# Strassen's method for most gate and up products of two FFNs in a decoder layer, and down products in three groups

## The chip, the cores and the metric

The kernel runs on one core of one Trainium2 chip. The metric is the device time of one execution in microseconds; before the change it is 1139.57 us, the median of three runs (1139.33 to 1140.59). The engines of the core are named as in the profile: PE multiplies matrices (PEld is its loading of weights), DVE, ACT and POOL work on vectors, SP issues transfers.

## The reference

One decoder layer on 512 tokens of width 1024, in float32. Two FFNs of width 2816 stand around a mixing part (two attention branches) that the change does not touch:

```python
def swiglu_ffn(x, g, w_gate, w_up, w_down):
    h = rms_norm(x, g)
    return (jax.nn.silu(h @ w_gate) * (h @ w_up)) @ w_down

x = x + 0.5 * swiglu_ffn(x, ffn1_norm, ffn1_w_gate, ffn1_w_up, ffn1_w_down)
...
x = x + merged @ w_out
x = x + 0.5 * swiglu_ffn(x, ffn2_norm, ffn2_w_gate, ffn2_w_up, ffn2_w_down)
```

## The kernel before

Everything lies transposed: a tile holds 128 features by 512 tokens. x has 8 such tiles (KD), the FFN's inner width 22 (KF). Every float32 matrix is split into a high part in PE's reduced format and the low rest, and a product of two is three matmuls (`mm3`, L110): high by high, high by low, low by high, all into one PSUM bank.

`load_w` (L97) brings a tile of weights: a transfer on SP's queue into one of three raw tiles (L104), a cast to the high part by ACT (L105), and the difference by DVE (L106; in the mixing part partly by POOL). Three buffers of high and low parts exist, so a tile can be split while two others wait or are used. PE's order is the order of the program; the other engines' instructions are put in order by the scheduler when the kernel is built.

`ffn` (L159) goes through the 22 feature tiles. For each it forms the gate product and the up product (`fm_product`, L151: 8 tiles of contraction, three matmuls of 512 columns each) against the split input `xh`, `xl`, which holds x times the gain without the norm's factor. `activate` (L165) then multiplies both by the norm's factor `rb` (L167, L170), takes the silu (L168), multiplies (L171) and splits the result into `ah` and `al` (L172, L173). PSUM has three banks for these products (`acc_tile`). The norm's statistics are computed by a few PE instructions in the second feature tile (`norm_stats`).

After all 22, the down products follow: for each of the 8 output tiles 22 x 3 matmuls, whose weights come in cuts of 8, 8 and 6 tiles (DOWN_CUTS), then half the sum is added to x (L216). In the second FFN the last output tile is done in two halves of 256 tokens, so that the first can leave while the second is computed; each finished tile is sent out at once (L770). After the first FFN each finished tile of x goes through `prep` (L115) for the mixing part.

A gate or up product and a down cut of 8 are each 24 matmuls.

Of the kernel before, what the change touches and what calls it, by code (L numbers as in the profile page):

```python
# [2 lines left out]

# [1 line left out]

# [6 lines left out]
F32 = mybir.dt.float32  # L12
F32R = mybir.dt.float32r
# [5 lines left out]
P = 128  # L19
T = 512  # L20
# [18 lines left out]
BIG = 1e30  # L39
S_W = 208  # L40
GA = ("g_ffn1", "g_mix", "g_ffn2")
DOWN_CUTS = ((0, 8), (8, 16), (16, 22))


@with_exitstack
def tile_hybrid_layer(ctx: ExitStack, tc: tile.TileContext, a: dict):
# [2 lines left out]

    ctx.enter_context(tc.manual_schedule(engines={mybir.EngineType.PE}))  # L50
    const = ctx.enter_context(tc.tile_pool(name="const", bufs=1))
    wpool = ctx.enter_context(tc.tile_pool(name="wpool", bufs=3))
    tmp = ctx.enter_context(tc.tile_pool(name="tmp", bufs=6))
    small = ctx.enter_context(tc.tile_pool(name="small", bufs=4))
# [2 lines left out]
    def acc_tile(name):  # L57
        return psum.tile([P, T], F32, tag="acc", bufs=3, name=name)
# [26 lines left out]
    hg = const.tile([P, 4], F32, name="hg")  # L85
    bf = const.tile([P, H], F32, name="bf")

    const.tile([P, 8], F32, name="before_x")
    xh = [const.tile([P, T], F32R, name=f"xh{d}") for d in range(KD)]
    xl = [const.tile([P, T], F32R, name=f"xl{d}") for d in range(KD)]  # L90
    const.tile([P, 56], F32, name="behind_x")
    ssq = [None]
    lo_eng = [V]
    first = None


    def load_w(src, n, m, raw=None):  # L97
        f = n * m
        if raw is None:
            raw = wpool.tile([P, 1024], F32, tag="raw", bufs=3, name="raw")  # L100
        wh = wpool.tile([P, 1024], F32R, tag="wh", name="wh")
        wl = wpool.tile([P, 1024], F32R, tag="wl", name="wl")
        with tc.high_priority(offset=1 if first else 30):
            nc.sync.dma_start(raw[:, :f].rearrange("p (n m) -> p n m", n=n), src)  # L104
            S.copy(wh[:, :f], raw[:, :f])  # L105
            lo_eng[0].tensor_sub(wl[:, :f], raw[:, :f], wh[:, :f].bitcast(F32))  # L106
        return (wh[:, :f].rearrange("p (n m) -> p n m", n=n),
                wl[:, :f].rearrange("p (n m) -> p n m", n=n))

    def mm3(out, lh, ll, rh, rl, start, stop):  # L110
        PE.matmul(out, lh, rh, start=start, stop=False)  # L111
        PE.matmul(out, lh, rl, start=False, stop=False)  # L112
        PE.matmul(out, ll, rh, start=False, stop=stop)  # L113

    def prep(d, gi):  # L115

        g = gains[:, gi, d:d + 1]
        S.mul(xh[d], x[d], g)
        V.scalar_tensor_tensor(xl[d], x[d], g, xh[d].bitcast(F32), op0=OP.mult, op1=OP.subtract)

# [13 lines left out]
    def norm_stats():  # L134

        ps = psum.tile([P, T], F32, tag="pt", bufs=2, name="ps_ssq")
        for t in range(NT):
            PE.matmul(ps[:, t:t + 1], ssq[0][:, t * P:(t + 1) * P], ones[:, 0:1], start=True, stop=True)
        v = small.tile([P, NT], F32, tag="v", name="v")
        V.tensor_scalar(v, ps[:, 0:NT], 1.0 / D, EPS, op0=OP.mult, op1=OP.add)  # L140
        r = small.tile([P, NT], F32, tag="rstd", bufs=2, name="rstd")
        G.tensor_tensor(r, v, nhalf[:, 0:NT], op=OP.pow)
        yield r
        pb = psum.tile([P, T], F32, tag="pt", bufs=2, name="ps_rb")
        for t in range(NT):
# [11 lines left out]
        return ps  # L157

    def ffn(n, nxt, parts=lambda d: [slice(0, T)]):  # L159
        wg, wu, wd = a[f"w_gate{n}"], a[f"w_up{n}"], a[f"w_down{n}"]  # L160
        with tc.tile_pool(name=f"ffn{n}", bufs=1) as ap:
            ah = [ap.tile([P, T], F32R, name=f"ah{n}_{f}") for f in range(KF)]
            al = [ap.tile([P, T], F32R, name=f"al{n}_{f}") for f in range(KF)]

            def activate(f, pg, pu, rb):  # L165
                g = tmp_tile("g")
                V.tensor_mul(g, pg, rb)  # L167
                S.activation(g, g, AF.Silu)  # L168
                u = tmp_tile("u")
                V.tensor_mul(u, pu, rb)  # L170
                V.tensor_mul(u, u, g)  # L171
                S.copy(ah[f], u)  # L172
                V.tensor_sub(al[f], u, ah[f].bitcast(F32))  # L173

            stats = norm_stats()
            rb = None
            held = []
            mid = {1: lambda: next(stats), 4: lambda: held.append(next(stats))}
            for f in range(KF):
                if f == 0 and first:  # L180
                    pg, pu = acc_tile("pg"), acc_tile("pu")
                    for k in range(KD):
                        for ps, w in zip((pg, pu), first):
                            PE.matmul(ps, w[k][0], xh[k], start=k == 0, stop=False)
                            PE.matmul(ps, w[k][1], xh[k], start=False, stop=False)
                            PE.matmul(ps, w[k][0], xl[k], start=False, stop=k == KD - 1)
                else:
                    pg = fm_product(load_w(wg[f], KD, P), "pg", mid if f == 1 and n == 2 else {})
                if f == 1 and n == 2:
                    activate(0, *pair0, held[0])  # L190
                    rb = held[0]
                if f == 0 and first:
                    first.clear()
                elif f == 1 and n == 1:

                    pu = fm_product(load_w(wu[f], KD, P), "pu", mid, psum.tile([P, T], F32, tag="s", bufs=2, name="pu1"))
                    activate(0, *pair0, held[0])
                    rb = held[0]
                else:
                    pu = fm_product(load_w(wu[f], KD, P), "pu")  # L200
                if f == 0:
                    pair0 = (pg, pu)
                else:
                    activate(f, pg, pu, rb)
            for d in range(KD):
                ws = []

                for cols in parts(d):
                    ps = acc_tile("pd")[:, cols]
                    for c, (lo, hi) in enumerate(DOWN_CUTS):  # L210
                        if c == len(ws):
                            ws.append(load_w(wd[d][:, lo:hi], hi - lo, P))
                        for k in range(lo, hi):
                            mm3(ps, ws[c][0][:, k - lo], ws[c][1][:, k - lo], ah[k][:, cols], al[k][:, cols],
                                k == 0, k == KF - 1)
                    V.scalar_tensor_tensor(x[d][:, cols], ps, 0.5, x[d][:, cols], op0=OP.mult, op1=OP.add)  # L216
                    nxt(d, cols)


    first = [[], []]  # L220
# [553 lines left out]
def _fm(w):  # L774

    k, n = w.shape
    return w.reshape(k // P, P, n // P, P).transpose(2, 1, 0, 3)
# [22 lines left out]
def _layout(x, ffn1_norm, ffn1_w_gate, ffn1_w_up, ffn1_w_down, mix_norm, w_in, b_forget,  # L800
            fox_q_norm, fox_k_norm, dsa_q_norm, dsa_k_norm, rel_bias,
            w_branch_a, w_branch_b, w_out, ffn2_norm, ffn2_w_gate, ffn2_w_up, ffn2_w_down):
    o = {}
    o["x"] = x.reshape(T, KD, P).transpose(2, 1, 0)
    o["gains"] = np.stack([g.reshape(KD, P).T for g in (ffn1_norm, mix_norm, ffn2_norm)], axis=1)
    o["hgain"] = np.stack([np.concatenate([g, g]) for g in (fox_q_norm, dsa_q_norm, fox_k_norm, dsa_k_norm)], axis=1)
    o["bforget"] = np.broadcast_to(b_forget, (P, H))
    for n, (g, u, dn) in ((1, (ffn1_w_gate, ffn1_w_up, ffn1_w_down)), (2, (ffn2_w_gate, ffn2_w_up, ffn2_w_down))):
        o[f"w_gate{n}"] = _fm(g)
        o[f"w_up{n}"] = _fm(u)  # L810
# [35 lines left out]
```

## Time and profile before

| what | us |
|---|---|
| median of three runs | 1139.57 |
| the profiled execution | 1139.26 |
| its span, first to last instruction | 1137.5 |
| mean granted PE clock, share of full | 0.998 |

The span is made up of the first FFN (to about 366 us), the mixing part (to about 780) and the second FFN. In a stage table each row is a stretch of the span, with every engine's busy time in it and the count of its instructions in brackets; then come the granted clock, the mean busy share of the DMA engines, and GB/s. In a group row stand line, engine, operation, tiles and shapes, the count, then busy us and mean ns of one, then the idle time of the engine just before them and what ended it. A timeline row is start in us, duration in us, engine, line and operation. Matmuls overlap in PE's pipeline, so that the duration of one is longer than the distance from its start to the next one's.

### The profile page before, as it was taken

What the parts mean: (1) busy time and instruction counts of PE and PEld (TensorE: products, weight loads), DVE (VectorE), ACT (ScalarE), POOL (GpSimd) and SP (SyncE); (2) the same over time, 40 slices, a digit from 0 to 9 for tenths busy, and PEclk for the clock granted to TensorE, in tenths of its full rate; (3) what the DMA queues carried; (4) which work ended last, traced back from release to release, by engine and by line L of the source; (5) the groups of instructions that cost most, each with busy time, mean ns of one, the idle gap of its engine ahead of it and who ended that gap; (6) DMA issues with size and microseconds to landing.
All of it is one profiled execution on the core that took longest, in us unless ns stands there. A gap on an engine that the chain in (4) does not pass through costs nothing.

```text
span 1137.5 us, 14491 instructions
## 1 busy us (share of the span) xinstructions
PE 1122.8 (99%) x5560; PEld 942.7 (83%) x5560; DVE 598.8 (53%) x1028; ACT 455.0 (40%) x742; POOL 190.8 (17%) x235
## 2 busy tenths in 40 slices
PE   8999999999999999999999999999999999999998
PEld 6888888888888898888888778888888888888888
DVE  6544444443332489987765765854544445432221
ACT  6322332232222654667755775443322233222210
POOL 0000000000001438676853540000000000000000
PEclk9999999999999999999999999999999999999999
DMA  6233222323332222222123211422223332233340
GB/s 223 93 99 103 95 93 93 109 86 102 90 100 84 90 75 95 74 74 76 47 56 130 84 65 45 147 97 93 93 93 96 101 99 93 93 97 108 120 120 19
DMA packets 34069, 106.69 MB, mean 94 GB/s; under 512 B 4168, under 2 KB 4552, under 8 KB 34000
## 3 DMA queue, kind: packets, MB, share of 16 engines
q1 hardware_dynamic: 33856, 105.50, 29.1%
q8 instruction: 44, 0.72, 0.3%
q10 hardware_dynamic: 144, 0.26, 0.1%
q14 instruction: 25, 0.20, 0.1%
HBM read 103.63 MB, written 2.11 MB: 93 GB/s over the span
## 4 chain that ended last, share of the span: by engine, by line
PE 86%; DVE 7%; ACT 3%; issue 2%; POOL 1%; DMA 1%; SPq 0%; DVEq 0%; POOLq 0%; ACTq 0%
PE pd L113 7%; PE pd L112 7%; PE pd L111 7%; PE pg L113 7%; PE pu L111 7%; PE pu L113 7%; PE pg L111 7%; PE pu L112 7%; PE pg L112 7%; PE ps_f L111 2%; PE ps_f L112 2%; PE ps_f L113 2%; PE ps_t L111 2%; DVE sc L525 1%; PE ps_out L112 1%
## 5 line engine op out<-in xcount | busy, mean ns | idle before, releaser
L105 ACT CAST wh<-raw 128x1024 fp32r<-128x1024 f32 (+3 forms) x200 | 198.0, 991 | 534.0 <-issue 216.9
L106 DVE TENSOR_TENSOR wl<-raw,wh 128x1024 fp32r<-128x1024 f32 (+3 forms) x182 | 215.0, 1182 | 151.6 <-ACT wh L105 151.2
L112 PE MATMUL pd<-al,wh 128*128 128x512 f32 (+1 forms) x374 | 140.8, 377 | 0.0
L113 PE MATMUL pd<-ah,wl 128*128 128x512 f32 (+1 forms) x374 | 140.8, 377 | 0.0
L111 PE MATMUL pd<-ah,wh 128*128 128x512 f32 (+1 forms) x374 | 140.8, 377 | 0.0
L113 PE MATMUL pg<-xh,wl 128*128 128x512 f32 x344 | 134.0, 389 | 0.6 <-DVE wl L106 0.6
L111 PE MATMUL pg<-xh,wh 128*128 128x512 f32 x344 | 134.1, 390 | 0.0
L111 PE MATMUL pu<-xh,wh 128*128 128x512 f32 x344 | 134.0, 390 | 0.0
L113 PE MATMUL pu<-xh,wl 128*128 128x512 f32 x344 | 133.9, 389 | 0.0
L112 PE MATMUL pg<-xl,wh 128*128 128x512 f32 x344 | 133.9, 389 | 0.0
L112 PE MATMUL pu<-xl,wh 128*128 128x512 f32 x344 | 133.8, 389 | 0.0
L106 POOL TENSOR_TENSOR wl<-raw,wh 128x1024 fp32r<-128x1024 f32 (+1 forms) x18 | 42.4, 2355 | 372.3 <-ACT wh L105 372.3
L170 DVE TENSOR_TENSOR u<-pu,rb 128x512 f32<-128x512 f32 x44 | 30.4, 691 | 134.9 <-PE pu L113 134.9
L111 PE MATMUL ps_t<-wh,xh 128*128 128x256 f32 (+1 forms) x288 | 84.9, 295 | 0.0
L112 PE MATMUL ps_t<-wl,xh 128*128 128x256 f32 (+1 forms) x288 | 81.9, 284 | 0.0
L113 PE MATMUL ps_t<-wh,xl 128*128 128x256 f32 (+1 forms) x288 | 81.8, 284 | 0.0
L112 PEld LDWEIGHTS pd<-al,wh 128*128 128x128 f32 x374 | 70.4, 188 | 13.0
L111 PEld LDWEIGHTS pd<-ah,wh 128*128 128x128 f32 x374 | 70.4, 188 | 12.9
L113 PEld LDWEIGHTS pd<-ah,wl 128*128 128x128 f32 x374 | 70.4, 188 | 12.7
L113 PEld LDWEIGHTS pg<-xh,wl 128*128 128x128 f32 x344 | 64.5, 188 | 14.4 <-DVE wl L106 1.0
L167 DVE TENSOR_TENSOR g<-pg,rb 128x512 f32<-128x512 f32 x44 | 30.4, 691 | 86.8 <-PE pg L113 86.6
L113 PEld LDWEIGHTS pu<-xh,wl 128*128 128x128 f32 x344 | 64.6, 188 | 13.6
(204 smaller groups left out, 2003.5 us busy)
## 6 DMA issues: line engine op xcount, KB each, us to landing
raw<-in_w_gate_dram SPq DMA_DIRECT2D x43, 512.0 KB, 3.4
raw<-in_w_up_dram SPq DMA_DIRECT2D x43, 512.0 KB, 3.5
raw<-in_w_down_dram SPq DMA_DIRECT2D x32, 512.0 KB, 3.5
raw<-in_w_down_dram SPq DMA_DIRECT2D x16, 384.0 KB, 3.1
raw<-in_w_ga_dram SPq DMA_DIRECT2D x8, 512.0 KB, 3.4
raw<-in_w_gb_dram SPq DMA_DIRECT2D x8, 512.0 KB, 3.2
raw<-in_w_out_dram SPq DMA_DIRECT2D x8, 512.0 KB, 3.3
raw<-in_w_iq_dram SPq DMA_DIRECT2D x4, 512.0 KB, 3.3
```

The lines of the kernel that those rows point to most:

```text
L105: S.copy(wh[:, :f], raw[:, :f])
L106: lo_eng[0].tensor_sub(wl[:, :f], raw[:, :f], wh[:, :f].bitcast(F32))
L111: PE.matmul(out, lh, rh, start=start, stop=False)
L112: PE.matmul(out, lh, rl, start=False, stop=False)
L113: PE.matmul(out, ll, rh, start=False, stop=stop)
L167: V.tensor_mul(g, pg, rb)
L170: V.tensor_mul(u, pu, rb)
L525: V.match_replace(out=sc[i], in_to_replace=m8, in_values=sc[i], imm_value=-3e38)
```

## The change

Feature tiles 0 to 5 are computed as before. Tiles 6 to 21 are taken in 8 pairs. For a pair, gate and up are each a product of a weight block (two feature tiles by two halves of the contraction) and the input (two halves of the contraction by two halves of the tokens). In place of the eight products of quarters, seven are formed (the form of Strassen's method with fewer sums): their weights are the quarters a, b, c, d or sums of them, their moving parts are halves of x or sums of them. Each of the seven steps holds gate and up (m) and four tiles of contraction (k), with 256 columns: 24 matmuls. Some accumulate onto an earlier product in the same bank.

The moving parts (`b1`, `b2`, `ta`, `tb`) are formed once per FFN by `combine`, from x times gain times the norm's factor, in the plain steps after the factor is known, two parts after each step. The sums of weights (s1, s2, S3, S4) are formed by DVE ahead of their cast. A pair's quarters come in four raw tiles, ra, rb, rc and a new one, rd; loads are listed in order on SP and issued as tiles come free, splits are written two steps ahead of their step. The activations of a pair need no multiplication by the norm's factor. For most tiles the low part is now made as minus the high part (ACT) plus an accumulating DMA from POOL's queue; the last pair of each group (and tiles 0 and 1) has DVE's difference.

The FFN is done in three groups of feature tiles (8, 8, 6); after each, its part of the down products for all 8 output tiles is formed and added to x. In a group the last pair's first tile, which is finished last, is read last. Only the last group of the second FFN keeps the halved last tile. The tiles of `xh` and `xl` lie in a pool of their own, whose places serve the pairs once the plain steps are done.

```diff
-DOWN_CUTS = ((0, 8), (8, 16), (16, 22))
+GROUPS = ((0, 8), (8, 16), (16, 22))
+PLAIN = 6
+HT = T // 2
+HK = KD // 2
...
+    def stream(i, dtype, name):
+        return xpool.tile([P, 2 * T], dtype, tag=f"X{i}", name=name)
...
+    def raw_tile(tag):
+        return wpool.tile([P, 1024], F32, tag=tag, bufs=1, name=tag)
+    def split_w(raw, f=1024):
+        wh = wpool.tile([P, 1024], F32R, tag="wh", name="wh")
+        wl = wpool.tile([P, 1024], F32R, tag="wl", name="wl")
+        S.copy(wh[:, :f], raw[:, :f])
+        V.tensor_sub(wl[:, :f], raw[:, :f], wh[:, :f].bitcast(F32))
+        return wh, wl
...
+        if d % 2 == 0:
+            for i, (part, nm) in enumerate(((xh, "xh"), (xl, "xl"))):
+                t = stream(HK * i + d // 2, F32R, nm)
+                part[d], part[d + 1] = t[:, :T], t[:, T:]
...
+            def act_tiles(f):
+                q, lo = f // 2, next(lo for lo, hi in GROUPS if lo <= f < hi)
+                j = q - lo // 2
+                if q not in act:
+                    act[q] = ([ap.tile([P, 2 * T], F32R, tag=f"a{j}{i}", name=f"a{i}") for i in "hl"]
+                              if j < 3 else [stream(6 + i, F32R, "ax") for i in range(2)])
+                return [t[:, f % 2 * T:f % 2 * T + T] for t in act[q]]
+            def split_act(f, u, late):
+                h, l = act_tiles(f)
+                S.copy(h, u)
+                if late:
+                    S.mul(l, h.bitcast(F32), -1.0)
+                    G.dma_start(l, u, accum_op=OP.add)
+                else:
+                    V.tensor_sub(l, u, h.bitcast(F32))
...
-                S.copy(ah[f], u)
-                V.tensor_sub(al[f], u, ah[f].bitcast(F32))
+                split_act(f, u, 1 < f < PLAIN)
...
+            def combine(k):
+                xn = ap.tile([P, 2 * T], F32, tag="rd", name="xn")
+                lo, hi = xn[:, :T], xn[:, T:]
+                for dst, d in ((lo, k), (hi, k + HK)):
+                    V.scalar_tensor_tensor(dst, x[d], gains[:, gi, d:d + 1], rbs[0], op0=OP.mult, op1=OP.mult)
+                split_to("b1", k, lo[:, :HT], HT)
+                yield
+                ta, tb = tmp_tile("ta"), tmp_tile("tb")
+                V.tensor_sub(ta[:, :HT], lo[:, :HT], lo[:, HT:])
+                V.scalar_tensor_tensor(tb[:, :HT], ta[:, :HT], -1.0, hi[:, HT:], op0=OP.mult, op1=OP.subtract)
+                V.tensor_sub(ta[:, HT:], hi[:, HT:], lo[:, HT:])
+                V.scalar_tensor_tensor(tb[:, HT:], tb[:, :HT], -1.0, hi[:, :HT], op0=OP.mult, op1=OP.subtract)
+                split_to("tb", k, tb)
+                yield
+                split_to("ta", k, ta)
+                split_to("b2", k, hi)
+                yield
...
-            for d in range(KD):
-                ws = []
-                for cols in parts(d):
-                    ps = acc_tile("pd")[:, cols]
-                    for c, (lo, hi) in enumerate(DOWN_CUTS):
-                        if c == len(ws):
-                            ws.append(load_w(wd[d][:, lo:hi], hi - lo, P))
-                        for k in range(lo, hi):
-                            mm3(ps, ws[c][0][:, k - lo], ws[c][1][:, k - lo], ah[k][:, cols], al[k][:, cols],
-                                k == 0, k == KF - 1)
-                    V.scalar_tensor_tensor(x[d][:, cols], ps, 0.5, x[d][:, cols], op0=OP.mult, op1=OP.add)
-                    nxt(d, cols)
...
+            def plain(src, f, run):
+                def split(st):
+                    return [t[:, :f * P].rearrange("p (n m) -> p n m", n=f) for t in split_w(raws[st.tag], f * P)]
+                return Step([(None, f, src)], split, run)
...
+                def product(bank, w, b, start):
+                    wh, wl = (z.rearrange("p (m k c) -> p m k c", m=2, k=HK) for z in w)
+                    for m in range(2):
+                        for k in range(HK):
+                            mm3(bank[:, m * HT:(m + 1) * HT], wh[:, m, k], wl[:, m, k], b[0][:, k], b[1][:, k],
+                                start and m == 0 and k == 0, m == 1 and k == HK - 1, skip_group_check=not start)
+                def finish(f, gu):
+                    S.activation(gu[:, 0], gu[:, 0], AF.Silu)
+                    V.tensor_mul(gu[:, 1], gu[:, 1], gu[:, 0])
+                    split_act(f, gu[:, 1], not last)
...
+                def split_a(st):
+                    t["s1"] = stream(0, F32, "s1")
+                    V.tensor_add(t["s1"], raws["rc"], raws["rd"])
+                    return split_w(raws["ra"])
+                def split_s2(st):
+                    t["s2"] = stream(1, F32, "s2")
+                    V.tensor_add(t["s2"], t["s1"], raws["ra"])
+                    return split_w(t["s2"])
+                def split_s3(st):
+                    V.tensor_add(raws["rc"], raws["rc"], raws["ra"])
+                    return split_w(raws["rc"])
+                def split_s4(st):
+                    V.tensor_add(t["s2"], t["s2"], raws["rb"])
+                    return split_w(t["s2"])
+                def run_a(w):
+                    t["A"] = acc_tile("pA")
+                    product(t["A"], w, moving("b1", 0), True)
+                    t["c1"] = tmp_tile("c1")
+                    S.copy(t["c1"], t["A"])
+                def run_s2(w):
+                    t["B"] = acc_tile("pB")
+                    product(t["B"], w, moving("tb", 0), True)
+                    t["u2"] = tmp_tile("u2")
+                    V.tensor_add(t["u2"], t["B"], t["c1"])
+                def run_s1(w):
+                    t["C"] = acc_tile("pC")
+                    product(t["C"], w, moving("ta", 0), True)
+                def run_s3(w):
+                    product(t["B"], w, moving("ta", 1), False)
+                    u3 = tmp_tile("u3")
+                    V.tensor_add(u3, t["B"], t["c1"])
+                    t["gu1"], t["gu2"] = gu_tile(), gu_tile()
+                    V.scalar_tensor_tensor(t["gu2"][:, :, HT:], view(t["C"]), -1.0, view(u3), op0=OP.mult, op1=OP.subtract)
+                def run_b(w):
+                    product(t["A"], w, moving("b2", 0), False)
+                    S.copy(t["gu1"][:, :, :HT], view(t["A"]))
+                def run_d(w):
+                    product(t["B"], w, moving("tb", 1), False)
+                    V.scalar_tensor_tensor(t["gu2"][:, :, :HT], view(t["B"]), -1.0, view(t["c1"]), op0=OP.mult, op1=OP.subtract)
+                    finish(2 * q + 1, t["gu2"])
+                def run_s4(w):
+                    product(t["C"], w, moving("b2", 1), False)
+                    V.tensor_add(t["gu1"][:, :, HT:], view(t["C"]), view(t["u2"]))
+                    finish(2 * q, t["gu1"])
+                src = [wp[q - PLAIN // 2, i] for i in range(4)]
+                return [Step([("rc", 0, src[2]), ("rd", 0, src[3]), ("ra", 0, src[0])], split_a, run_a),
+                        Step([], split_s2, run_s2),
+                        Step([("rb", 0, src[1])], lambda st: split_w(t["s1"]), run_s1),
+                        Step([], split_s3, run_s3, ("ra", "rc")),
+                        Step([], lambda st: split_w(raws["rb"]), run_b),
+                        Step([], lambda st: split_w(raws["rd"]), run_d, ("rd",)),
+                        Step([], split_s4, run_s4, ("rb",))]
+            def run_down(d, lo, hi):
+                def run(w):
+                    order = [k for k in range(hi - lo - 2)] + [hi - lo - 1, hi - lo - 2]
+                    end = hi == KF
+                    for cols in parts(d) if end else [slice(0, T)]:
+                        ps = acc_tile("pd")[:, cols]
+                        for k in order:
+                            h, l = act_tiles(lo + k)
+                            mm3(ps, w[0][:, k], w[1][:, k], h[:, cols], l[:, cols], k == order[0], k == order[-1])
+                        V.scalar_tensor_tensor(x[d][:, cols], ps, 0.5, x[d][:, cols], op0=OP.mult, op1=OP.add)
+                        if end:
+                            nxt(d, cols)
+                return run
+            steps = []
+            gu_at = cycle(range(4))
+            for lo, hi in GROUPS:
+                for f in range(lo, min(hi, PLAIN)):
+                    if f or not first:
+                        steps += [plain(wg[f], KD, run_gate(f)), plain(wu[f], KD, run_up(f))]
+                for q in range(max(lo, PLAIN) // 2, hi // 2):
+                    steps += pair_steps(q, 2 * q + 2 == hi)
+                steps += [plain(wd[d][:, lo:hi], hi - lo, run_down(d, lo, hi)) for d in range(KD)]
...
+            def look_ahead(i):
+                for j in range(i, min(i + 3, len(steps))):
+                    if j not in ws:
+                        while queue and queue[0][0] <= j:
+                            load()
+                        ws[j] = steps[j].split(steps[j])
+                        free.update(steps[j].frees)
+                        if steps[j].tag:
+                            free.add(steps[j].tag)
+                while queue and queue[0][0] <= i + 6 and (queue[0][1][0] or free - {"rd"}) and (
+                        queue[0][1][0] is None or queue[0][1][0] in free):
+                    load()
+            for i, st in enumerate(steps):
+                look_ahead(i)
+                st.run(ws[i])
+                if rbs and combos:
+                    for _ in range(2):
+                        if next(combos, "end") == "end":
+                            combos = None
+                            free.add("rd")
```

The order in which the weights lie in memory is changed to fit (a pair's quarters, gate and up together); the bytes that are loaded stay the same.

More of the change, by code (lines that the diff above doesn't have):

```diff
@@ L1 @@
 from contextlib import ExitStack, nullcontext
-from itertools import chain
+from itertools import chain, cycle
 import numpy as np
@@ L86, in tile_hybrid_layer @@
     bf = const.tile([P, H], F32, name="bf")
[L88 to L91, printed above, removed]
+    xh, xl = [None] * KD, [None] * KD
+    def stream(i, dtype, name):
+        return xpool.tile([P, 2 * T], dtype, tag=f"X{i}", name=name)
     ssq = [None]
@@ L94, in tile_hybrid_layer @@
     first = None
+    raw_tags = cycle(("ra", "rb", "rc"))
+    def raw_tile(tag):
[6 more added lines that the diff above has]
+        return wh, wl
     def load_w(src, n, m, raw=None):
@@ L99, in load_w @@
         if raw is None:
-            raw = wpool.tile([P, 1024], F32, tag="raw", bufs=3, name="raw")
+            raw = raw_tile(next(raw_tags))
         wh = wpool.tile([P, 1024], F32R, tag="wh", name="wh")
@@ L108, in load_w, with mm3 @@
                 wl[:, :f].rearrange("p (n m) -> p n m", n=n))
[L110 to L113, printed above, removed]
+    def mm3(out, lh, ll, rh, rl, start, stop, **more):
+        PE.matmul(out, lh, rh, start=start, stop=False, **more)
+        PE.matmul(out, lh, rl, start=False, stop=False, **more)
+        PE.matmul(out, ll, rh, start=False, stop=stop, **more)
     def prep(d, gi):
         g = gains[:, gi, d:d + 1]
+        if d % 2 == 0:
+            for i, (part, nm) in enumerate(((xh, "xh"), (xl, "xl"))):
+                t = stream(HK * i + d // 2, F32R, nm)
+                part[d], part[d + 1] = t[:, :T], t[:, T:]
         S.mul(xh[d], x[d], g)
@@ L159, in ffn @@
     def ffn(n, nxt, parts=lambda d: [slice(0, T)]):
-        wg, wu, wd = a[f"w_gate{n}"], a[f"w_up{n}"], a[f"w_down{n}"]
+        wg, wu, wp, wd = (a[f"w_{nm}{n}"] for nm in ("gate", "up", "pair", "down"))
+        gi = 0 if n == 1 else 2
         with tc.tile_pool(name=f"ffn{n}", bufs=1) as ap:
-            ah = [ap.tile([P, T], F32R, name=f"ah{n}_{f}") for f in range(KF)]
-            al = [ap.tile([P, T], F32R, name=f"al{n}_{f}") for f in range(KF)]
+            act = {}
+            def act_tiles(f):
[13 more added lines that the diff above has]
+                    V.tensor_sub(l, u, h.bitcast(F32))
             def activate(f, pg, pu, rb):
@@ L171, in activate, with parts_tile, operand @@
                 V.tensor_mul(u, u, g)
-                S.copy(ah[f], u)
-                V.tensor_sub(al[f], u, ah[f].bitcast(F32))
+                split_act(f, u, 1 < f < PLAIN)
+            def parts_tile(nm, cols):
+                return [ap.tile([P, HK * cols + 64], F32R, tag=nm + i, name=nm + i)[:, 8:8 + HK * cols]
+                        .rearrange("p (k t) -> p k t", k=HK) for i in "hl"]
+            ops = {}
+            def operand(nm, cols=T):
+                if nm not in ops:
+                    ops[nm] = parts_tile(nm, cols)
+                return ops[nm]
@@ new lines, in split_to @@
+            def split_to(nm, k, src, cols=T):
+                h, l = (t[:, k] for t in operand(nm, cols))
+                S.copy(h, src)
+                V.tensor_sub(l, src, h.bitcast(F32))
+            def combine(k):
[15 more added lines that the diff above has]
+                yield
@@ L175, in ffn, with moving @@
+            def moving(nm, half):
+                h, l = ops[nm]
+                sl = slice(half * HT, half * HT + HT)
+                return (h, l) if nm == "b1" else (h[:, :, sl], l[:, :, sl])
+            combos = chain(*(combine(k) for k in range(HK)))
+            held, pair0, rbs = [], [], []
             stats = norm_stats()
-            rb = None
-            held = []
             mid = {1: lambda: next(stats), 4: lambda: held.append(next(stats))}
[L179 to L204, printed above, removed]
@@ L205, in ffn, with __init__ @@
[L205 to L217 removed]
+            class Step:
+                def __init__(self, loads, split, run, frees=()):
+                    self.loads, self.split, self.run, self.frees = loads, split, run, frees
+                    self.tag = None
@@ new lines, in run_up, with run @@
+            def run_up(f):
+                def run(w):
+                    if f == 1 and n == 1:
+                        pu = fm_product(w, "pu", mid, psum.tile([P, T], F32, tag="s", bufs=2, name="pu1"))
+                        activate(0, *pair0, held[0])
+                        rbs.append(held[0])
+                    else:
+                        pu = fm_product(w, "pu")
+                    if f == 0:
+                        pair0.extend((pg[0], pu))
+                    else:
+                        activate(f, pg[0], pu, rbs[0])
+                return run
@@ new lines, in pair_steps, with view, gu_tile @@
+            def pair_steps(q, last):
+                t = {}
+                def view(ps):
+                    return ps.rearrange("p (m t) -> p m t", m=2)
+                def product(bank, w, b, start):
[8 more added lines that the diff above has]
+                    split_act(f, gu[:, 1], not last)
+                def gu_tile():
+                    return stream(2 + next(gu_at), F32, "gu").rearrange("p (m t) -> p m t", m=2)
+                def split_a(st):
[50 more added lines that the diff above has]
+                        Step([], split_s4, run_s4, ("rb",))]
@@ new lines, in run_down, with run @@
+            def run_down(d, lo, hi):
+                def run(w):
+                    order = [k for k in range(hi - lo - 2)] + [hi - lo - 1, hi - lo - 2]
[8 more added lines that the diff above has]
+                            nxt(d, cols)
+                return run
@@ new lines, in ffn @@
+            if first:
+                pg[0], pu = acc_tile("pg"), acc_tile("pu")
+                for k in range(KD):
+                    for ps, w in zip((pg[0], pu), first):
+                        PE.matmul(ps, w[k][0], xh[k], start=k == 0, stop=False)
+                        PE.matmul(ps, w[k][1], xh[k], start=False, stop=False)
+                        PE.matmul(ps, w[k][0], xl[k], start=False, stop=k == KD - 1)
+                first.clear()
+                pair0.extend((pg[0], pu))
@@ new lines, in ffn, with load @@
+            queue = [(i, ld) for i, st in enumerate(steps) for ld in st.loads]
+            ws, used = {}, []
+            def load():
+                i, (tag, f, src) = queue.pop(0)
+                if tag is None:
+                    tag = steps[i].tag = max(sorted(free - {"rd"}), key=lambda z: used[::-1].index(z) if z in used else len(used))
+                free.remove(tag)
+                used.append(tag)
+                raws[tag] = ap.tile([P, 1024], F32, tag="rd", name="rd") if tag == "rd" else raw_tile(tag)
+                nc.sync.dma_start(raws[tag][:, :f * P].rearrange("p (n m) -> p n m", n=f) if f else raws[tag], src)
```

15 lines of the change are left out of this document (13 added, 2 removed).

## The prediction

> **What bounds the kernel now.** I read the page first, for the busy shares and the chain that ended last.
>
> ```profile
> span 1137.5 us, 14491 instructions
> PE 1122.8 (99%) x5560; PEld 942.7 (83%) x5560; DVE 598.8 (53%) x1028; ACT 455.0 (40%) x742; POOL 190.8 (17%) x235
> PE 86%; DVE 7%; ACT 3%; issue 2%; POOL 1%; DMA 1%; SPq 0%; DVEq 0%; POOLq 0%; ACTq 0%
> ```
>
> PE is busy nearly everywhere and 86% of the chain is its matmuls. But the share is a mean over stages, so next comes the table by stage: gate and up products of the first FFN, its down products, the same gate and up products of the second, and two stretches of the mixing part between.
>
> ```profile
> core 0: us, PE busy (x) PEld busy (x) DVE busy (x) ACT busy (x) POOL busy (x), PEclk, DMA share, GB/s
> 31.00:249.00 218.00, 218.00 (x963) 180.51 (x962) 103.74 (x125) 66.93 (x83) 0.00 (x0) 1.00 0.29 95
> 250.00:366.00 116.00, 116.00 (x513) 96.08 (x512) 39.56 (x45) 32.11 (x39) 1.98 (x1) 1.00 0.32 95
> 790.00:1009.00 219.00, 219.00 (x968) 181.33 (x967) 103.12 (x124) 67.23 (x83) 0.00 (x0) 1.00 0.30 96
> 420.00:560.00 140.00, 134.32 (x964) 120.97 (x963) 122.13 (x332) 88.73 (x185) 102.43 (x128) 0.99 0.23 75
> 560.00:770.00 210.00, 207.79 (x1001) 170.81 (x1002) 137.84 (x272) 121.55 (x231) 62.92 (x84) 1.00 0.27 87
> ```
>
> In the FFNs PE has no idle time at all, the granted clock is 1.00, DVE works less than half of the time (103.74 of 218 us), ACT a third, POOL not at all, and the DMA engines 0.3. So an FFN lasts as long as its matmuls take to issue, and DVE has room. What counts is the time from the start of one matmul to the start of the next, not the duration of one. The timeline gives it for 512 columns (down products) and for 256 (the two halves of the last down tile):
>
> ```profile
> 299.85 0.39 PE L113 MATMUL pd<-ah,wl 128*128 128x512 f32 x1
> ...
> 303.93 0.39 PE L113 MATMUL pd<-ah,wl 128*128 128x512 f32 x1
> ...
> 1118.21 0.28 PE L111 MATMUL pd<-ah,wh 128*128 128x256 f32 x1
> ...
> 1133.92 0.28 PE L113 MATMUL pd<-ah,wl 128*128 128x256 f32 x1
> ...
> L111 PE MATMUL pd<-ah,wh 128*128 128x256 f32 x44 | 12.4, 283 | 0.0
> ```
>
> From 299.85 to 303.93 there are 18 steps: 4.08 / 18 = 0.2267 us for 512 columns. From 1118.21 to 1133.92 there are 44 on each of three lines, 132 matmuls and 131 steps: 15.71 / 131 = 0.1199 us, call it 0.120, for 256. Half the columns cost 53%, not 50%: the difference, 0.1067 us for 256 columns, makes 0.2134 for 512, so each matmul pays about 13 ns whatever its width. Every one of them loads new weights, as those of the change will.
>
> **The matmuls of a pair.** Two feature tiles of gate and up are now four products of 8 x 3 matmuls of 512 columns: 96 x 0.2267 = 21.76 us. Strassen's seven products, each of 2 x 4 x 3 matmuls of 256 columns, are 168 x 0.120 = 20.16 us. An eighth of the columns goes (2.69 us by column count), but the 13 ns are paid 72 times more; 1.60 us remain. With 8 pairs in each of two FFNs: 16 x 1.60 = 25.6 us less.
>
> The Trainium skill, page "TensorE: Matmul & The Clock Gate", section "Back-to-back issue gap", gives N / 2.4 + 2.5 ns: 215.8 and 109.2 ns. By it a pair would save 20.72 - 18.35 = 2.37 us and the change 37.9; the rows show five times that fixed part, in both widths, and the sum goes by the rows.
>
> **The down products in groups.** The same 528 matmuls per FFN, over 8, 8 and 6 feature tiles. The last tile's halving now touches only the 6 of the last group: 16 x 3 matmuls stay whole, 48 x (2 x 0.120 - 0.2267) = 0.6 us less, once. The 16 more additions to x per FFN are DVE's and lie beside matmuls.
>
> **What DVE and ACT get.** This decides whether the 1.60 us arrive. Durations come from the groups of the two FFN stages, by form, and two of the mixing part:
>
> ```profile
> L106 DVE TENSOR_TENSOR wl<-raw,wh 128x1024 fp32r<-128x1024 f32 x40 | 48.9, 1221 | 4.2 <-ACT wh L105 4.2
> L170 DVE TENSOR_TENSOR u<-pu,rb 128x512 f32<-128x512 f32 x21 | 14.5, 691 | 62.9 <-PE pu L113 62.9
> L173 DVE TENSOR_TENSOR al<-u,ah 128x512 fp32r<-128x512 f32 x21 | 14.4, 685 | 0.1
> L119 DVE SCALAR_TENSOR_TENSOR xl<-x,gains,xh 128x512 fp32r<-128x512 f32 x7 | 5.2, 745 | 0.0
> L592 DVE TENSOR_TENSOR pl<-pt,ph 128x256 fp32r<-128x256 f32 x16 | 6.7, 419 | 2.4 <-ACT ph L591 1.9
> L105 ACT CAST wh<-raw 128x1024 fp32r<-128x1024 f32 x40 | 42.2, 1054 | 133.4 <-issue 73.6 <-PE pg L112 59.8
> L172 ACT CAST ah<-u 128x512 fp32r<-128x512 f32 x21 | 13.1, 625 | 13.9 <-DVE u L171 13.9
> ...
> L591 ACT CAST ph<-pt 128x512 fp32r<-128x512 f32 x16 | 9.3, 582 | 5.1 <-PE po L597 4.2 <-PE pt L587 0.8
> ```
>
> DVE per pair: seven low halves of weights and four sums of weight quarters, 11 x 1.22 = 13.4 us; u2, u3, three combinations out of PSUM and two products with the silu, 7 x 0.69 = 4.8 us; together 18.3 of 20.16 us (now 4 x 1.22 + 8 x 0.69 = 10.4 of 21.76). ACT: 7 x 1.05, two copies out of PSUM at 0.58, two silus, casts and negations, 6 x 0.625: 12.3 us. POOL issues two accumulating DMAs. So DVE goes from half busy to 91%, in order, with sums, casts and differences hanging on each other. I worked one pair through by hand, a product each 2.88 us. Split j may start when product j-3 gives back its buffers, 5.76 us before it is needed, and takes 1.05 + 1.22 after its sum; the sums need no buffer and fit into earlier gaps; u2 and u3 have one product (2.88 us) before their bank is written again. Put in order of readiness, everything comes out at least 1 us before it is needed and DVE keeps 1.5 to 2 us idle. The tightest loop goes through raw tile rd: landed, two sums (2.44), cast and difference (2.27) to the second product; two products on (5.76) buffers for the split of rd itself (2.27), then the reload:
>
> ```profile
> raw<-in_w_gate_dram SPq DMA_DIRECT2D x43, 512.0 KB, 3.4
> ```
>
> With 0.4 for the issue that is 2.44 + 2.27 + 5.76 + 2.27 + 3.8 = 16.5 us of 20.16: 3.6 to spare, which DVE's queue eats first. The other loads wait behind rd's on SP, and are needed later.
>
> What a crowded DVE costs PE has only distant rows: the stretch 420 to 560, DVE 122.13 of 140 us busy (87%), where PE lost 140 - 134.32 = 5.7 us (4%), and 560 to 770 (66%), where it lost 2.2 of 210 (1%). Softmax chains go through PE there, and here no product waits for the one before it. On 16 x 20.16 = 323 us these are 13 and 3 us; below nothing is excluded, since PE can't issue faster than its pitch. I take 3, nearest the hand schedule, and keep 0 to 13.
>
> **Combining x.** Once per FFN, within six of the plain products (5.44 us each), DVE forms the moving halves: 4 x (2 x 0.745 + 3 x 0.685 + 5 x 0.42) = 22.6 us, 3.8 a product, beside a split (1.22) and half an activation (1.04): 6.0 in 5.44. It falls 3.5 us behind over six products, with splits two products ahead (10.9 us less 2.3 of cast and difference), and catches up in the three after them. I take 0.5 per FFN; bounds 0 and 3.5.
>
> **The ends of the groups.** Now no down product waits for a fresh activation, since the last tile is read last of 22. After the change each group's last pair is read soon. Its chain after product 7, by the rows: 0.3 for the last matmul to end (0.28 above), then 0.69, 0.625, 0.69, 0.625, 0.69 with one cast (1.05) between: some 5 us. The order of the down product puts that tile last: after 7 x 3 x 0.2267 = 4.8 us in the groups of 8 (even), after 5 x 3 x 0.2267 = 3.4 us in the group of 6: 1.2 us late if one cast stands between, 3 if a difference of 1.22 and another cast do. I take 1.2 per FFN, bounds 0 and 4 (all three groups).
>
> The activations whose low half comes by DMA are read at least a pair and two tiles of the down product later, 20.16 + 1.4 us, less the 5 us chain: 16 us after the issue, which covers it; the rest of the program keeps its instructions. A tail of x's last half and its way out stays the same.
>
> **The sum.** 1137.5 - 25.6 - 0.6 + 3 + 2 x 0.5 + 2 x 1.2 = 1117.7 us of span. The profiled execution took 1139.26 in all, 1.76 beyond its span: 1119.5 us. It lay 0.3 below the median of 1139.57.
>
> **The rivals.** *DVE slowed by POOL.* One difference in the mixing part shows what a shared path does:
>
> ```profile
> 503.21 2.51 DVE L106 TENSOR_TENSOR wl<-raw,wh 128x1024 fp32r<-128x1024 f32 x1
> ...
> 503.57 1.06 POOL L386 TENSOR_TENSOR kn<-kn,rh 128x512 f32<-128x512 f32 x1
> ```
>
> 2.51 us in place of 1.22, while POOL worked on tiles of its own. If each of the two accumulating DMAs of a pair holds one such instruction up by 1.29 us, DVE needs 18.3 + 2.6 = 20.9 us, 0.7 more than the matmuls; 16 x 0.7 = 11 in place of 3: 1127.5 us. For it: the 9% of room are no more than this. Against: POOL only issues there, it reads no tile. The Trainium skill, page "SBUF — State Buffer", section "SBUF: two separate sides", puts a DMA's descriptors from POOL under the lock of a port that it shares with DVE, but for DVE's two-port modes; no run here shows one. Chance 0.17, with all cases between 1125 and 1134.
>
> *DVE becomes the bound* (slower than before). If DVE's order puts nothing between a sum's cast and its difference, three casts (3.2 us) and two silus (1.25) stand open in each pair: 18.3 + 4.4 = 22.7 us, 2.5 over the matmuls, 16 x 2.5 = 40 in place of 3: 1156.5 us. It decides from 20.16 + (26.2 - 3.4) / 16 = 21.6 us a pair. For it: before, DVE's longest waits in the gate stage are for PE and it never had to interleave there. Against: at 87% busy in 420 to 560 it did, and in the hand schedule other ready work lies in these gaps. Chance 0.09.
>
> *The fixed part is not paid.* If narrow matmuls out of one bank issued at their columns alone, 0.107 us, the pair would take 17.9 us: 16 x 2.2 = 35 us less again, 1084; half of that, 1102. The rows at 1118 to 1134 speak against it: the same form, the same bank, 0.120. The skill's formula above, 12.3 us more than mine, would give 1107. Chance 0.05 for all under 1112.
>
> *No change*, the gain eaten to within 2.3 us: 0.03.
>
> **How the numbers follow.** The forecast, 1112 to 1125, has 0.66. The range goes from 1112.5 (all costs at nothing: 1113.1) to 1132, which takes in most of the first rival. About 0.2% (2.3 us) is what a measurement of this kernel can tell from no change; faster by more: 0.66 + 0.17 + 0.05 = 0.88, within 0.03, slower 0.09.
>
> **What would show it.** Right: 256-column matmuls 0.120 us apart and pairs of 20.2 us; DVE at 80 to 91% in stretches of pairs; PE idle of a few us in all, most of it at the last tile of the group of 6, waiting for ACT or DVE. Wrong: gaps before each product whose weights are a sum, released by DVE's difference (DVE the bound); differences of over 1.3 us in the pairs (POOL); waits for raw tiles (the rd loop); or another pitch.

## The result, and the profile after

The changed kernel takes 1121.25 us, the median of four runs (1120.59 to 1123.0), beside 1139.49 before in the same series: a ratio of 0.984, 95% interval 0.9823 to 0.9857. The forecast was 1119.5. The profiled execution took 1123.0 us with a span of 1121.0 and is thus the slowest of the four; compared with the profile before, its span is 16.5 us shorter.

From the page after: the first lines, the transfer queue that is new (the accumulating DMAs), and the chain:

```profile
span 1121.0 us, 17245 instructions
...
PE 1095.7 (98%) x6664; PEld 966.5 (86%) x6664; DVE 776.1 (69%) x1240; ACT 549.8 (49%) x882; POOL 215.9 (19%) x263
...
q0 software_dynamic: 4032, 7.34, 3.9%
...
PE 75%; DVE 12%; DMA 4%; ACT 4%; issue 3%; POOL 1%; SPq 0%; DVEq 0%; POOLq 0%; ACTq 0%
```

PE's share of the chain fell from 86 to 75%, DVE's rose from 7 to 12, and DMA has 4% that were 1: something now waits for a transfer. The stage table says where. Its rows are the one pair of the first group and the four pairs of the second group in the first FFN:

```profile
75.23:94.83 19.60, 19.60 (x169) 19.60 (x168) 14.86 (x16) 9.98 (x12) 0.85 (x1) 1.00 0.54 149
138.57:158.17 19.60, 19.60 (x169) 19.60 (x168) 13.98 (x15) 8.33 (x9) 0.00 (x0) 1.00 0.25 82
158.17:177.77 19.60, 19.60 (x170) 19.60 (x169) 14.13 (x16) 10.64 (x14) 1.72 (x2) 1.00 0.52 135
177.77:199.05 21.28, 20.48 (x170) 19.90 (x169) 16.40 (x19) 11.25 (x15) 1.72 (x2) 1.00 0.45 124
199.05:221.13 22.08, 20.37 (x170) 19.79 (x169) 18.98 (x21) 12.92 (x17) 1.70 (x2) 1.00 0.52 144
```

The first pairs take 19.60 us, less than the 20.16 that were worked out; the third and fourth in a row take 1.7 and 2.5 us more, while DVE is not full. The second FFN repeats it (in the two FFNs, six pairs of sixteen are long, 16.1 us together over 16 x 19.60). What holds them up is in the chain of waits at the start of the third pair of the second group (start us, us, what; "issue" is here the rest of the first sum, L331):

```profile
166.66 1.06 ACT wh L112
...
167.74 1.24 DVE wl L113
...
168.99 6.50 DMA rd<-in_w_pair_dram
...
175.51 0.06 DVE s L331
175.58 1.08 issue
176.66 1.22 DVE wl L113
177.88 1.13 DVE s L336
179.01 1.14 DVE rc L340
180.15 0.60 DVE gu L376
180.75 1.14 DVE wl L113
...
181.93 0.39 PE pB L132
```

It reads as one loop: the cast and the difference of rd (from 167.74) release its tile, the reload takes 6.50 us, and then DVE does the first sum, which reads rd, the difference of ra, the second sum, the third sum and a combination of PSUM before the difference for which product 2 waits. The next reload of rd begins at 190.75 in the same chain, 21.76 us after this one: longer than a pair, so every further pair in a row is late.

In short, by spans: the pairs' matmuls 16 x (21.76 - 19.60) = 34.6 us less, the halves of the last tile 0.6 less, the long pairs 16.1 more, the ends of the groups 2.6 more: 16.5, as measured. The other stages differ by some tenths either way.

### The profile page after: what moved, and what is told of

The parts are those of the page before. It is cut to its first block, busy times and chain, and to the rows that moved or that the text cites. A ratio compares the mean times of both kernels' runs of the same rounds, so it can differ in the third digit from the quotient of the medians.

```text
span 1121.0 us, 17245 instructions
## 1 busy us (share of the span) xinstructions
PE 1095.7 (98%) x6664; PEld 966.5 (86%) x6664; DVE 776.1 (69%) x1240; ACT 549.8 (49%) x882; POOL 215.9 (19%) x263
## 4 chain that ended last, share of the span: by engine, by line
PE 75%; DVE 12%; DMA 4%; ACT 4%; issue 3%; POOL 1%; SPq 0%; DVEq 0%; POOLq 0%; ACTq 0%
PE pd L131 7%; PE pd L132 7%; PE pd L130 7%; DMA rd<-in_w_pair_dram 4%; PE pB L132 3%; PE pB L130 3%; PE pB L131 3%; PE ps_f L130 2%; PE ps_f L131 2%; PE ps_f L132 2%; DVE wl L113 2%; PE pC L131 2%; PE pC L130 2%; PE pg L132 2%; PE pu L130 2%
## 5 line engine op out<-in xcount | busy, mean ns | idle before, releaser
L112 ACT CAST wh<-s 128x1024 fp32r<-128x1024 f32 x48 | 49.9, 1052 | 110.3 <-DVE s L336 52.9
L112 ACT CAST wh<-ra 128x1024 fp32r<-128x1024 f32 (+1 forms) x42 | 42.9, 1022 | 115.0 <-PE pd L131 42.0
L132 PE MATMUL pB<-tbh,wl 128*128 128x256 f32 x256 | 72.1, 281 | 4.6 <-DVE wl L113 4.6
L130 PE MATMUL pB<-tbh,wh 128*128 128x256 f32 x256 | 71.9, 281 | 0.8
L131 PE MATMUL pB<-tbl,wh 128*128 128x256 f32 x256 | 71.4, 279 | 0.0
L112 ACT CAST wh<-rc 128x1024 fp32r<-128x1024 f32 (+1 forms) x41 | 41.7, 1018 | 60.3 <-PE pd L131 28.5
L113 DVE TENSOR_TENSOR wl<-s,wh 128x1024 fp32r<-128x1024 f32 x48 | 58.3, 1219 | 1.7 <-ACT wh L112 1.7
L130 PEld LDWEIGHTS ps_t<-wh,xh 128*128 128x128 f32 x288 | 55.3, 192 | 4.6 <-issue 3.0
L113 DVE TENSOR_TENSOR wl<-rc,wh 128x1024 fp32r<-128x1024 f32 (+1 forms) x41 | 48.6, 1185 | 14.9 <-ACT wh L112 14.9
L131 PEld LDWEIGHTS ps_t<-wl,xh 128*128 128x128 f32 x288 | 55.4, 192 | 0.2
```

Source lines behind the costliest of these rows:

```text
L113: V.tensor_sub(wl[:, :f], raw[:, :f], wh[:, :f].bitcast(F32))
L130: PE.matmul(out, lh, rh, start=start, stop=False, **more)
L131: PE.matmul(out, lh, rl, start=False, stop=False, **more)
L132: PE.matmul(out, ll, rh, start=False, stop=stop, **more)
```

## The experiments

All edits are to the changed kernel. Before's median on the same chip was 1139.9 to 1140.3 us in these series.

**A second place for rd.** My theory was now the reload loop; the rival that DVE, crowded, sets the pace. In the diffs "..." stands for lines left out: here the list of free tiles, the tiles' names, and that the combining of x uses the first of the two places.

```diff
...
+                rd = f"rd{q % 2}"
...
-                    V.tensor_add(t["s1"], raws["rc"], raws["rd"])
+                    V.tensor_add(t["s1"], raws["rc"], raws[rd])
...
-                return [Step([("rc", 0, src[2]), ("rd", 0, src[3]), ("ra", 0, src[0])], split_a, run_a),
+                return [Step([("rc", 0, src[2]), (rd, 0, src[3]), ("ra", 0, src[0])], split_a, run_a),
...
-                        Step([], lambda st: split_w(raws["rd"]), run_d, ("rd",)),
+                        Step([], lambda st: split_w(raws[rd]), run_d, (rd,)),
...
```

> A second place for raw tile rd, pairs taking the two in turn; all work the same. Theory (the stalls of about 16 us in consecutive pairs come from the reload of rd, which may start only after the split of rd itself and took 6.5 us where it was costed at 3.8): the reload is out of the loop, PE's waits at the pairs' first three products nearly vanish, and the time falls by 12 to 16 us, to 1105 to 1109. Rival (DVE, with 17 to 18 us of work in 19.6, is the bound in consecutive pairs): DVE's work is the same, the stalls stay, 1119 to 1122.

Measured: 1107.67 us (1107.07 to 1108.54), ratio to before 0.9717 (0.9701 to 0.9733). The four pairs of the second group, as one row of its stage table:

```profile
138.70:217.10 78.40, 78.40 (x674) 78.40 (x672) 64.12 (x67) 43.99 (x55) 5.10 (x6) 1.00 0.46 129
```

78.40 = 4 x 19.60, PE without a gap, and all sixteen pairs are like that, with the same work on DVE (64.12 of 78.40 us, 82%). So the loop through rd was the whole of the pairs' loss, and DVE was not the bound.

**No accumulating DMA.**

```diff
-                split_act(f, u, 1 < f < PLAIN)
+                split_act(f, u, False)
...
-                    split_act(f, gu[:, 1], not last)
+                    split_act(f, gu[:, 1], False)
```

> No accumulating DMA: the low half of every activation is DVE's difference; otherwise as the changed kernel. Theory (rd's reload is long because the accumulating DMAs of two activations share the DMA engines with it): rd lands in 4 to 5 us instead of 6.5, the loop is 2 us shorter and the six stalled pairs give back 6 to 10 us: 1112 to 1116, though DVE has 1.4 us more per pair. Rival (DVE is the bound): 10 pairs with 1.4 us more of DVE's work are slower by up to 14 us: 1125 to 1135. Rival two (loads among themselves make the reload long): within 3 us of 1121.

Measured: 1106.95 us (1106.74 to 1107.64), 0.9712 (0.9697 to 0.9726): more than the theory expected, though rd has one place and DVE more work. rd's time from issue to landing, least, median and most of 16, of the changed kernel and then of this one:

```profile
DMA to landing us min/median/max: 3.4/4.7/8.6
```

```profile
DMA to landing us min/median/max: 3.2/3.8/4.5
```

The pairs take 19.60 us (one 19.73). With a reload of 3.8 us the loop of 21.76 us would be some 19.1 (an estimate), which fits in a pair; the accumulating DMAs are what made the reload long. Their own rows, from the changed kernel's page (KB each, us to landing):

```profile
rd<-in_w_pair_dram SPq DMA_DIRECT2D x16, 512.0 KB, 4.7
...
al<-gu POOLq DMA_DIRECT2D x20, 256.0 KB, 6.6
```

Half the bytes took 6.6 us. Two of them were issued from 166.31 on, just ahead of the load of rd for the third pair, on POOL and on SP of the changed kernel:

```profile
166.31 1.72 POOL L203 DMA_DIRECT2D al<-gu  x2 [82.61 <-DVE wl L113]
...
164.60 0.33 SPq L438 DMA_DIRECT2D rc<-in_w_pair_dram  x1
166.33 0.33 SPq L438 DMA_DIRECT2D rb<-in_w_pair_dram  x1
168.99 0.33 SPq L438 DMA_DIRECT2D rd<-in_w_pair_dram  x1
```

The same holds for all sixteen loads of rd in that trace: the eight that follow two accumulating DMAs within 3 us took 5.3 to 8.6 us, the other eight 3.4 to 4.2. Could the loads of rc and rb just ahead of rd have made it long by themselves? Without the accumulating DMAs the three loads stand as close:

```profile
165.16 0.33 SPq L438 DMA_DIRECT2D rc<-in_w_pair_dram  x1
167.50 0.33 SPq L438 DMA_DIRECT2D rb<-in_w_pair_dram  x1
169.53 0.33 SPq L438 DMA_DIRECT2D rd<-in_w_pair_dram  x1
```

This load of rd took 4.3 us. It goes both ways: in the kernel with two places for rd, where the loads of rd mostly stand apart from them, the same twenty accumulating DMAs took 4.0 us in the median. The edit removes one more thing, ACT's negations, of which 0.62 us stands in the chain ahead of the cast of rd in the next loop (187.91); how much of the gain is theirs was not measured apart.

**Both together.**

> Two places for rd and no accumulating DMA together. Theory (one cause, the reload of rd made long by the accumulating DMAs; either edit removes it): nothing is left to gain, 1106 to 1108, pairs of 19.6 us. Rival (each edit removed a part of its own): below 1105.

Measured: 1108.07 us (1107.22 to 1109.38), 0.9722 (0.9707 to 0.9736): no further gain, all pairs at 19.60. The two edits remove one and the same wait. Each of the three runs beats the kernel before and the changed one; which of them is the fastest can't be told from these runs.

**The place of the moving operand.** The pitch in the pairs, 19.60 / 168 = 0.1167 us, was not the 0.120 of the rows before. The moving halves of x lie 32 bytes behind the start of their tiles.

```diff
-                return [ap.tile([P, HK * cols + 64], F32R, tag=nm + i, name=nm + i)[:, 8:8 + HK * cols]
+                return [ap.tile([P, HK * cols + 64], F32R, tag=nm + i, name=nm + i)[:, :HK * cols]
```

> The moving halves of x begin at the start of their tiles, not 32 bytes behind it. If the place of the moving operand makes the pitch of 0.1167 us (0.120 in the halved down tile, where the operand has no such shift), the pitch goes to 0.120, a clean pair from 19.6 to 20.2 us, and the time up by 5 to 9 us. If the shift has nothing to do with it: 0.1167 and 1121 as before.

Measured: 1125.92 us (1121.83 to 1126.78), 0.987 (0.9851 to 0.989). The pitch is read from the timeline: matmuls of a first pair stand 0.12 apart, and the twelve pairs that the reload loop does not hold up take 20.15 to 20.16 us, in place of 19.60:

```profile
140.23 0.28 PE L131 MATMUL pA<-b1l,wh 128*128 128x256 f32 x1
140.35 0.28 PE L132 MATMUL pA<-b1h,wl 128*128 128x256 f32 x1
```

The time, 4.7 us over that of the changed kernel, is just under the 5 to 9 that were expected, and it does not come from the pitch. The sixteen pairs took 329.7 us together in this profile and 329.7 in that of the changed kernel, because only four pairs are long here and not six. The 2.3 us by which the span is longer lie outside the pairs, 1.3 of them in the mixing part, and I didn't follow them.

With the shift doubled (16 elements in place of 8):

> The moving halves of x begin 64 bytes behind the start of their tiles in place of 32. If what counts is the place within 64 bytes: 0.120 us apart as with no shift, 1124 to 1127. If what counts is that the operand does not begin where its tile does: 0.1167 us and 1121.

Measured: 1120.89 us (1120.57 to 1121.84), 0.9834 (0.9818 to 0.9851); a clean pair takes 19.79 us, 0.1178 a matmul. That is neither of the two pitches that were expected, but one between them: the place within 64 bytes alone does not decide, nor does the mere fact of a shift. What of the operands' places does, these runs leave open.

**The groups alone**, with PLAIN at 22, nothing combined, natural order of the tiles and DVE's differences:

> The groups alone: all 22 tiles of gate and up plain as in the kernel before, no combining of x, no pairs; the down products in three groups, in natural order, all low halves by DVE. Theory (the groups cost nothing by themselves but a wait at the end of a group): 1138 to 1141, with 0.6 us less for the last tile's halves. Rival (the groups cost several us in handovers, which then hide in the sum of the change): 1143 or more.

Measured: 1141.36 us (1140.88 to 1143.54), 1.0016 (1.0007 to 1.0025): 0.4 us above the theory's range and short of the rival's. The two FFNs last as before (the first 0.6 us more, the second 0.3 less); the mixing part, whose instructions are unchanged, lasted 3.8 us longer in its profile, which is that of the slowest of ten runs. In the changed kernel it lasted only 0.3 us longer than before. So the groups cost next to nothing in the FFNs; the rest I didn't follow.

**More work for DVE.** If the loop was the whole loss, DVE had room. First, sums of a tile with itself, two or four a pair, on the kernel with two places for rd (one of the places is shown):

```diff
...
+            def more():
+                V.tensor_add(dz, dz, dz)
...
-                        Step([("rb", 0, src[1])], lambda st: split_w(t["s1"]), run_s1),
+                        Step([("rb", 0, src[1])], lambda st: (more(), split_w(t["s1"]))[1], run_s1),
...
```

> Two places for rd, and in each pair two more sums of 128x1024 on DVE that nobody reads (written ahead of the splits of products 3 and 6); output unchanged. DVE's work per pair goes from 17 us (17.22 busy in a pair of 19.6) to 19.3. Theory (DVE packs its work nearly without holes and bounds a pair only when its sum passes 19.6 us): at most 4 us over the kernel with two places for rd (1107.7), so 1107 to 1112. Rival (a DVE over 90% busy already holds PE up, 4% of the pairs' time and more): 1119 to 1130.

> As the run with two more sums, but four per pair: DVE's work is 21.6 us per pair, 2.0 us over the matmuls. Theory (past 19.6 us DVE is the bound, less what it can work ahead at the start of each group): 10 to 32 us over 1107.7, so 1118 to 1140. Rival (in-order waits leave holes, so it costs the holes too): over 1145.

Measured: 1128.52 us (1126.74 to 1129.37), 0.9898 (0.9883 to 0.9913), and 1147.58 us (1146.95 to 1150.18), 1.0072 (1.0057 to 1.0087). The numbers fit the rivals, but not for their reason. In the timeline of the first the sums stand far ahead of the pairs:

```profile
61.64 1.21 DVE L262 TENSOR_TENSOR dz<-dz 128x1024 f32<-128x1024 f32 x1
62.77 0.41 DVE L246 SCALAR_TENSOR_TENSOR tb<-tb,xn 128x256 f32<-128x256 f32 x1
63.11 1.21 DVE L113 TENSOR_TENSOR wl<-ra,wh 128x1024 fp32r<-128x1024 f32 x1
64.25 1.21 DVE L262 TENSOR_TENSOR dz<-dz 128x1024 f32<-128x1024 f32 x1
```

They wait for nothing, so the scheduler put them among the combining of x, where PE then stood for 10.2 us, waiting for DVE's product with the norm's factor:

```profile
72.35 0.76 PE L130 MATMUL pu<-xh,wh 128*128 128x512 f32 x1 [10.19 <-DVE g L209]
```

All pairs of the first run stayed at 19.60. As a probe of crowded pairs these two runs say nothing. They do say that DVE has little room left in the plain products. So again, with sums that read the pair's own s1 and s2:

```diff
...
+            def more(s):
+                V.tensor_add(dz, s, s)
...
                     V.tensor_add(t["s2"], t["s2"], raws["rb"])
+                    more(t["s2"])
...
-                        Step([("rb", 0, src[1])], lambda st: split_w(t["s1"]), run_s1),
+                        Step([("rb", 0, src[1])], lambda st: (more(t["s1"]), split_w(t["s1"]))[1], run_s1),
...
```

> As the run with two more sums per pair on DVE that nobody reads, but each now reads one of the pair's own sums of weights, so that it can't be moved out of its pair (there they were all moved ahead into the plain products). DVE's work per pair goes from 17 us to 19.3 of 19.6. Theory (DVE packs its work nearly without holes, and bounds a pair only past 19.6 us): 1107 to 1113. Rival (a DVE over 90% busy holds PE up): 1115 to 1130.

> The same with four more sums per pair, bound to the pair: DVE's work is 21.6 us, 2.0 over the matmuls. Theory (past 19.6 us DVE is the bound, less what it works ahead in the first pair of a group): 10 to 32 us over 1107.7, so 1118 to 1140. Rival (holes from in-order waits come on top): over 1145.

Measured: 1111.86 us (1111.45 to 1112.39), 0.9756 (0.974 to 0.9773), and 1122.57 us (1121.89 to 1123.08), 0.9848 (0.9834 to 0.9863); both times within the theory. The four pairs of the second group, two more sums and then four:

```profile
139.20:218.70 79.50, 79.17 (x673) 78.91 (x672) 69.85 (x73) 43.40 (x55) 5.14 (x6) 1.00 0.46 127
```

```profile
140.20:222.30 82.10, 79.81 (x674) 78.95 (x673) 77.68 (x81) 43.97 (x55) 5.09 (x6) 1.00 0.44 123
```

At 69.85 of 79.50 us (88%) the pairs lose 0.3 us each on average; at 77.68 of 82.10 (95%) 0.9 each. That is some 1 and 5% of PE's time in a pair. DVE worked ahead: of the eight and sixteen sums of these four pairs two and three were done before the rows begin, during the down products. So in neither run did DVE have more work inside the pairs than the matmuls take, as had been expected of the second.

## Why the prediction was right, point by point

The time (1119.5, measured 1121.25) came out by luck: the way was right, but two terms were off in opposite ways, the matmuls by 9.0 us and the crowding by 13.1. Two of the signs that the prediction named for being wrong, another pitch and waits for a raw tile in the rd loop, did come.

*The matmuls of a pair.* The step was right in kind, the size too small: 2.16 us a pair in place of 1.60, 34.6 in place of 25.6. The pitch had been taken from the halved down tile, whose moving operand begins where its tile does; that row was the wrong neighbour, as the run without the shift shows (20.16 us, the figure of the sum). The formula of the Trainium skill, page "TensorE: Matmul & The Clock Gate", section "Back-to-back issue gap", has the pitch lower still, 0.1092; the page gives it for a single matmul apart from others, and no row or run here, all streams with weights of their own, reached it.

*What a crowded DVE costs.* The term of 3 us measured 16.1, over its upper bound of 13, and its cause was another one. The hand schedule had found the loop through rd and its slack of 3.6 us, but with the reload at 3.8 us, the issue and landing of a load that meets only loads of its own kind; it takes 6.5 where accumulating DMAs are under way. It also let DVE do the two sums at once, where three other instructions come between (176.66 to 180.75). Of the 5.2 us from the 16.5 that were worked out to 21.76, the transfer is 2.7, DVE's order 1.7, and the two products up to the cast of rd, with ACT's own queue ahead of it, 0.8. The sentence that the slack would be eaten first by DVE's queue was half right. DVE's work itself was put too high: 18.3 us of a pair, where the row of the kernel with two places for rd has 64.12 / 4 = 16.0, in part because differences and sums that follow each other begin 1.13 us apart and last 1.22. By itself its crowding cost nothing at 82% busy and 0.3 us a pair at 88%.

*DVE slowed by POOL* did not happen: differences in the pairs still last 1.22 us, and those at 187.60 and 189.50 took 1.22 each although POOL issued two accumulating DMAs from 188.30 to 190.02.

```profile
L113 DVE TENSOR_TENSOR wl<-s,wh 128x1024 fp32r<-128x1024 f32 x48 | 58.3, 1219 | 1.7 <-ACT wh L112 1.7
```

That agrees with the Trainium skill, page "SBUF — State Buffer", section "SBUF: two separate sides", where an operation of DVE with two inputs in SBUF shares the lock only against an operation of POOL that reads SBUF; the issue of a transfer reads no tile. *DVE the bound*, the slower side, would have needed 21.6 us of a pair; the kernel with four more sums, which comes to 20.5 on average, shows how far that was.

*Combining x*: no loss of PE found there, 1.0 forecast. The row of the plain products of the first FFN, where x is combined, has PE without a gap and DVE 94% busy, where more than 100% was expected (6.0 us of work in 5.44):

```profile
31.00:75.00 44.00, 44.00 (x195) 36.42 (x194) 41.44 (x68) 24.83 (x38) 2.76 (x3) 1.00 0.38 102
```

*The ends of the groups*: 2.4 forecast, 2.6 measured, and 1.7 of it where it was placed, at the last tile of the group of 6, here in the first FFN:

```profile
329.18 0.39 PE L132 MATMUL pd<-ah,wl 128*128 128x512 f32 x1
329.63 0.51 PE L130 MATMUL pd<-ah,wh 128*128 128x512 f32 x1
330.35 0.50 PE L131 MATMUL pd<-al,wh 128*128 128x512 f32 x1 [0.22 <-DVE al L205]
330.69 0.39 PE L132 MATMUL pd<-ah,wl 128*128 128x512 f32 x1
```

Three steps of 0.45, 0.72 and 0.34 us, where each takes 0.23: 0.83 us, waiting for the high and then the low half of the last activation.

## What to carry to other kernels

Work out every loop in which a buffer is refilled after its last use, and cost the refill with what else the DMA engines carry at that moment, not with the median of quiet loads: here a single place for one raw tile, or the choice of a DMA for a sum that DVE had time for, cost 14 us of a gain of 33. Take the pitch of a matmul from a row whose operands lie as those of the change will. A probe that adds work must read something of the stage that it is to burden, or the scheduler moves it elsewhere.

## What the runs showed of the hardware

Two things were not expected. A stream of matmuls of 256 columns, each with its own weights, was issued every 0.1200 us when the moving halves began at their tiles' start, every 0.1167 us with 32 bytes between, and every 0.1178 with 64. At 512 columns the gate products showed 0.227 us both before the change, where the kernel has a small tile of 32 bytes ahead of their operands, and after it, where it has none. And accumulating DMAs of 256 KB within SBUF took 6.6 us in the median from issue to landing when loads were issued beside them, and 4.0 where these mostly stood apart; a load of 512 KB issued within 3 us behind two of them took 5.3 to 8.6 us, and 3.4 to 4.2 otherwise.
